# Conv units as pairs of seven block products; gate and silu units beside the S5 layer

## The chip, the cores and the metric

One core of a Trainium2 chip runs one layer of a hybrid encoder on a sequence of 1024 tokens of width 1024, in fp32. The metric is the device time of one execution in microseconds (us). Before the change it is 1185.5 us, the median of three runs (1178.62, 1185.71 and 1185.5).

## The reference

The inner width of every unit is 1024. `u` goes through the S5 layer, 64 groups of 16 channels with complex diagonal states in both directions:

```
xn = RMSNorm(x)
u, z_a, v, b, c, z_b, g_a, g_b = split(xn @ W_in)          # eight units, 1024 x 1024 each
y  = gelu(S5(u));  y = y * sigmoid(y @ W_glu);  y_a = y * silu(z_a)
y_b = b * conv3(c * v) * silu(z_b)                          # 3 taps along the sequence
merged = sigmoid(g_a) * (y_a @ W_branch_a) + sigmoid(g_b) * (y_b @ W_branch_b)
out = RMSNorm(x + merged @ W_out)
```

## The kernel before

**Products.** An fp32 operand is kept as two fp32r tiles, a high part and the rest (`split`, L817: a CAST on ACT, a subtraction on DVE). A product of 128 output channels by 1024 positions is three passes (high x high, high x low, low x high) over eight blocks of 128 input channels and two halves of 512 positions: 48 matmuls of 128x512. Its weights are one load of 512 KB (`load_w`, L112).

**Pairs of seven.** Two neighbouring products (256 channels) can also be done as seven block products instead of eight (Strassen's scheme in Winograd's form): `seven` (L920 on) does B11, T2, T1, T3, B21, B22 and T4, 12 matmuls each, 84 instead of 96. For it the positions need sums and differences of blocks of xn (`sh`, `sl`, made once, L848 to L858), and the weights differences (`diff`, L899) that are split again; `prep` makes them for the next pair while this one runs. DVE's adds (`plus`, L943) put the products together in the tiles `go`. Each product has a PSUM tile of its own, from the pool `bg` of single banks (`bank`).

**Stages.** A prologue (norm, transposes, S5 tables, four units of `u`); then 46 products one after the other (`items`, run by `projections`), four for `u`, 32 for the conv (`conv_tile`: v, c, b and zb of each of eight channel blocks, finished on DVE and ACT right behind each), eight for za and two for gb; then seven pairs (the six other blocks of gb, all of ga); then the products ob, glu, oa and o.

**S5.** Between the products' blocks of six matmuls, S5's work is put in where a planner says that it is due: `ssm` yields one step at a time, `est` keeps its estimates of PE's and DVE's time, `part` queues a piece of PE work with the time from which it may go. Blocks n = 0 to 15 (four groups each) pass through: loads of U, bdt and pwt (512 KB each for the last two) and four DVE operations make the input map; `xps`, small matmuls, brings its product with U into SB; after four blocks, a scan of DVE operations (L666, L670); then `output_block` loads `ce`, makes W with six DVE operations (L618 to L620), `kf` and `kb` (L633, L636) make the kernel of the block, four small transfers `toe` turn it, and `yps` writes the output.

**Orders that matter below.** Each engine takes its instructions in the order of the program; SP issues all transfers in its own order, and an issue that waits holds those behind it. A tile of a pool is given again when its earlier use is over, and the program waits for that.

Of the kernel before, what the change touches and what calls it, by code (L numbers as in the profile page):

```python
# [52 lines left out]
def block_kernel(  # L53
# [46 lines left out]
    zsd = [dtile(f"zsd{i}", [P, D]) for i in range(K)]  # L100
    ctd = dtile("ctd", [P, NG // 4 * 192])
# [62 lines left out]
    with ExitStack() as st:  # L164
# [76 lines left out]


        def small(name, dt=F32, n=P):
            return pp.tile([NG, n], dt, tag=name, name=name)
# [6 lines left out]
        braw, craw = [], []  # L251
        for ri, (b, c) in enumerate(((ssm_b_re, ssm_c_re), (ssm_b_im, ssm_c_im))):
            bt = pp.tile([NG, 2, NG, H], F32, tag=f"braw{ri}", name=f"braw{ri}")
            nc.sync.dma_start(out=bt.rearrange("g d p h -> g d (p h)"), in_=b[0].rearrange("d g p h -> g d (p h)"))
            braw.append(bt)
            ct = pp.tile([P, K, 2, NG], F32, tag=f"craw{ri}", name=f"craw{ri}")
# [4 lines left out]
            craw.append(ct)  # L261
# [103 lines left out]
        Q = pp.tile([P, T + 1, 2, NG], F32, tag="Q", name="Q")  # L365
# [5 lines left out]
        qt1 = pp.tile([P, 4, NG], F32, tag="qt1", name="qt1")  # L371
        qt2 = pp.tile([P, 4, NG], F32, tag="qt2", name="qt2")
# [12 lines left out]
        Ein = pp.tile([P, T, 2, NG], F32, tag="Ein", name="Ein")  # L385
# [9 lines left out]
        bt1 = pp.tile([P, 8, NG], F32, tag="bt1", name="bt1")  # L395
        bt2 = pp.tile([P, 8, NG], F32, tag="bt2", name="bt2")
# [17 lines left out]
        R = pp.tile([P, L, 2, NG], F32, tag="R", name="R")  # L414
# [93 lines left out]
    def ssm(sp):  # L508
# [13 lines left out]
        def input_block():  # L522
            n = at["n"]
            q = n // 4
            if n % 4 == 0:
                SBs[q] = sp.tile([P, P, 2, GQ], F32, tag="SB", name=f"SB{q}", bufs=2)
# [4 lines left out]
            for src, outer, tag in ((bd, [[NG * 2 * P, H], [0, T]], "bdt"), (pw, [[0, H], [NG * 2 * P, T]], "pwt")):  # L531
                r_ = sp.tile([P, 4, 2, P], F32, tag=tag, name=f"{tag}_{nm}", bufs=2)
# [31 lines left out]
        def lags(b):  # L564
# [27 lines left out]
            b["out"] = part(est["dve"] + 4.0, 2.7, out_)  # L592

        def output_block(n, SB):
            gl = 4 * (n % 4)
            nm = f"y{n}"
            U = load_u(n, nm)
# [10 lines left out]
            Sx = sp.tile([P, 4, 2, P], F32, tag="Sx", name=f"Sx_{nm}")  # L608
            zsrc = SB[:, :, :, gl:gl + 4].rearrange("p k r g -> p g r k")
            G.memset(Sx[0:NG, :, :, 0:1], 0.0)  # L610
            G.memset(Sx[NG:P, :, :, P - 1:P], 0.0)
            S.copy(out=Sx[0:NG, :, :, 1:P], in_=zsrc[0:NG, :, :, 0:P - 1])  # L612
            S.copy(out=Sx[NG:P, :, :, 0:P - 1], in_=zsrc[NG:P, :, :, P - 2::-1])
# [9 lines left out]
            b = dict(nm=nm, n=n, U=U, Sx=Sx, W=W, out=None,  # L623
# [59 lines left out]
        def outputs():  # L683
            bs = []
            for n in range(NG // 4):
                while n // 4 not in scanned:
                    if bs and "done" not in bs[-1] and ready(bs[-1]["part"], 1.2):
                        lags(bs[-1])
                        bs[-1]["done"] = True
                        yield True  # L690
                    else:
                        yield False
                while len(bs) > 1 and not (bs[-2]["out"] and bs[-2]["out"]["end"] is not None):
                    yield False
                bs.append(output_block(n, SBs[n // 4]))
                if n % 4 == 3:
                    put_out.add(n // 4)
                yield True
                for b in bs[-2:] if n == NG // 4 - 1 else bs[-2:-1]:
                    while not ready(b["part"], 1.2):  # L700
                        yield False
                    if "done" not in b:
                        lags(b)
                        b["done"] = True
                    yield True
# [3 lines left out]
        while alive:  # L709
            for w in list(alive):  # L710
# [17 lines left out]
    def keep_u(i):  # L728
        def done(ps):
            us = t4(f"us{i}")  # L730
            S.copy(out=us, in_=ps)
            nc.sync.dma_start(out=ud[i], in_=us)
        return done

    def conv_tile(i):
        live = {}

        def v(ps):
            live["v"] = vs = t4(f"vs{i}")
            S.copy(out=vs, in_=ps)  # L740

        def c(ps):
            cv = t4(f"cv{i}")
            vec(5.3)
            V.tensor_tensor(out=cv, in0=ps, in1=live["v"], op=ALU.mult)
            live["acc"] = acc = t4(f"acc{i}")
            S.activation(out=acc, in_=cv, func=AF.Identity, scale=col(2, i), bias=col(4, i))
            w0, w2 = col(1, i), col(3, i)
            for w, do, so, n in ((w0, P, 0, 7 * P), (w0, 1, 7 * P, P - 1), (w2, 0, P, 7 * P), (w2, 7 * P, 1, P - 1)):
                V.scalar_tensor_tensor(out=acc[:, do:do + n], in0=cv[:, so:so + n], scalar=w,  # L750
                                       in1=acc[:, do:do + n], op0=ALU.mult, op1=ALU.add)

        def b(ps):
            vec(1.18)
            V.tensor_tensor(out=live["acc"], in0=ps, in1=live["acc"], op=ALU.mult)

        def zb(ps):
            sg, acc = t4(f"sgb{i}"), live["acc"]
            vec(3.0)
            S.activation(out=sg, in_=ps, func=AF.Sigmoid)  # L760
            V.tensor_tensor(out=sg, in0=ps, in1=sg, op=ALU.mult)
            V.tensor_tensor(out=acc, in0=acc, in1=sg, op=ALU.mult)
            nc.sync.dma_start(out=ybd[i], in_=acc)

        return [(wcol(2, i), v), (wcol(4, i), c), (wcol(3, i), b), (wcol(5, i), zb)]

    def za(i):
        def done(ps):
            sg = t4(f"sga{i}")
# [3 lines left out]
            nc.sync.dma_start(out=zsd[i], in_=sg)  # L773
# [7 lines left out]
    def gb(i):  # L781
        def done(ps):
            sg = t4(f"sgb{i}")
            S.activation(out=sg, in_=ps, func=AF.Sigmoid)
            nc.sync.dma_start(out=gbd[i], in_=sg)
        return done

    items += [(wcol(7, i), gb(i)) for i in range(2)]

    def projections():  # L790
        pair, done = load_w(items[0][0], "p0"), None
        for n, (w, next_done) in enumerate(items):
            ps = mm_tile(f"ps_p{n}")
            for k in range(K):
# [7 lines left out]
                if n + 1 == len(items) and k:  # L802
                    if k == 1:
                        late["first"] = load_pair(0)
                    elif 2 <= k <= 6:
                        while "S" not in late:
# [21 lines left out]
    late = {}  # L828
# [3 lines left out]
    def beside():  # L832
        with ExitStack() as own:
            sp = own.enter_context(tc.tile_pool(name="sp", bufs=2))
            yield from ssm(sp)
            while parts and not flush[0]:
                yield False
            put_parts(True)
        tabs.close()
        late["st"] = gs = ExitStack()  # L840
        sx = gs.enter_context(tc.tile_pool(name="sx", bufs=1))
        late["sw"] = gs.enter_context(tc.tile_pool(name="sw", bufs=1))
        late["S"] = {n: [] for n in "1234"}
        for k in range(HK):
            xs = []
# [5 lines left out]
            yield True  # L851
            for names, ops in (("31", ((xs[0], 0, xs[0], 1, ALU.subtract), (xs[0], 1, xs[1], 1, ALU.add))),
                               ("24", ((None, 1, xs[0], 0, ALU.subtract), (xs[1], 0, None, 0, ALU.subtract)))):
# [4 lines left out]
                h_ = sx.tile([P, D], F32R, tag=f"h{names}_{k}", name=f"sh{names}_{k}")  # L858
                l_ = sx.tile([P, D], F32R, tag=f"l{names}_{k}", name=f"sl{names}_{k}")
# [6 lines left out]
        for k in range(2):  # L866
            yt = t4(f"ybt{k}")
            nc.sync.dma_start(out=yt, in_=ybd[k])
            hi = tuple(xnh[2 * k + h][:, half[1]] for h in range(2))
            lo = tuple(xnl[2 * k + h][:, half[1]] for h in range(2))  # L870
            for h in range(2):
                split(yt[:, half[h]], hi[h], lo[h])
                vec(0.66)
            ybh.append(hi)
            ybl.append(lo)
            yield True

    pairs7 = [(7, i) for i in range(2, K, 2)] + [(6, i) for i in range(0, K, 2)]
# [17 lines left out]
    def diff(p, w, name, x_, y_):  # L896
        f_ = late["sw"].tile([P, HK, P], F32, tag="f4" if name == "T4" else "tf", name=f"f{name}_{p}",
                             bufs=1 if name == "T4" else 3)
# [27 lines left out]
    def seven(p, w):  # L926

        sx = late["S"]
# [239 lines left out]
```

## Time and profile before

| what | us |
|---|---|
| median of three runs | 1185.5 |
| the profiled execution | 1183.82 |
| its span | 1182.1 |
| PE busy | 1144.2 (97%) |
| DVE busy | 773.6 (65%) |
| ACT busy | 452.1 (38%) |
| mean granted TensorE clock | 0.993 of full speed |

All times are microseconds of one profiled execution. Busy is the union of an engine's instructions. In a timeline a row has its start, its length, engine, source line and operation, output and inputs, and in brackets how long the engine had stood idle before it and what ended that. The chain of waits follows the work that ended last back from the end. Matmuls are pipelined: a row of PE lasts longer than the distance to the next one.

### The profile page before, as it was taken

The page shows a single profiled execution, that of the slowest core. Times are in us where ns is not written, and L with a number is a line of the kernel's source. Part 1 is how long each engine was busy: PE and PEld are TensorE (multiplying, and loading weights), DVE is VectorE, ACT ScalarE, POOL GpSimd, SP SyncE. Part 2 cuts the span into 40 slices and gives each one's busy share as a digit, 9 for nine tenths or more (in the row PEclk, how much of TensorE's full clock was granted, in tenths as well). Part 3 has the DMA queues.
Part 4 walks back from the last instruction along what each step waited for, and adds up shares of the span by engine and source line. Part 5 has one row for each costly group of instructions (what it writes and reads, how often), then busy time and mean ns, then how long its engine had stood idle before and what let it go on. Part 6 is the DMA issues. An engine that isn't in the chain of part 4 may idle for free.

```text
span 1182.1 us, 14984 instructions
## 1 busy us (share of the span) xinstructions
PE 1144.2 (97%) x5842; PEld 948.1 (80%) x5842; DVE 773.6 (65%) x1220; ACT 452.1 (38%) x541; POOL 14.5 (1%) x59
## 2 busy tenths in 40 slices
PE   6999999998999999999999999999999999999997
PEld 4778888877788888878888878888788888887886
DVE  6854698884889959877955876564477325446244
ACT  6344752455314571433164343433344224223111
POOL 2000000000000000000000000000000000000000
PEclk9999999999999999999999999999999999999999
DMA  9249962146522462233344233427667424227012
GB/s 273 87 142 288 250 182 72 48 131 169 139 67 65 120 164 72 66 104 104 107 115 116 89 107 125 143 72 244 235 193 255 156 91 159 90 72 267 1 49 95
DMA packets 162427, 157.31 MB, mean 133 GB/s; under 512 B 11404, under 2 KB 138548, under 8 KB 162228
## 3 DMA queue, kind: packets, MB, share of 16 engines
q1 hardware_dynamic: 162212, 156.16, 43.3%
q8 instruction: 46, 0.75, 0.3%
q14 instruction: 25, 0.20, 0.0%
q10 hardware_dynamic: 144, 0.20, 0.0%
HBM read 114.39 MB, written 37.75 MB: 129 GB/s over the span
## 4 chain that ended last, share of the span: by engine, by line
PE 83%; DVE 6%; DMA 4%; ACT 3%; issue 2%; SPq 1%; POOL 0%; POOLq 0%; ACTq 0%; DVEq 0%
PE ps_p L134 35%; PE ps_glu L134 7%; PE o L1115 7%; PE ps_oa L134 7%; PE ps_ob L134 7%; PE gT L937 6%; PE gB L937 5%; PE xps_x L554 2%; PE ps_u L134 2%; PE yps_y L584 1%; PE yps_y L583 1%; PE yps_y L582 1%; DVE s L856 1%; DVE sl L819 1%; ACT sh L818 1%
## 5 line engine op out<-in xcount | busy, mean ns | idle before, releaser
L134 PE MATMUL ps_p<-xnh,wh_p 128*128 128x512 f32 x736 | 231.5, 396 | 0.0
L134 PE MATMUL ps_p<-xnl,wh_p 128*128 128x512 f32 x736 | 227.5, 390 | 0.0
L134 PE MATMUL ps_p<-xnh,wl_p 128*128 128x512 f32 x736 | 227.0, 390 | 0.0
L134 PEld LDWEIGHTS ps_p<-xnl,wh_p 128*128 128x128 f32 x736 | 138.4, 188 | 29.4
L134 PEld LDWEIGHTS ps_p<-xnh,wl_p 128*128 128x128 f32 x736 | 138.4, 188 | 29.1
L134 PEld LDWEIGHTS ps_p<-xnh,wh_p 128*128 128x128 f32 x736 | 135.4, 188 | 28.9 <-issue 3.2
L117 ACT CAST wh_p<-wr_p 128x1024 fp32r<-128x1024 f32 x46 | 48.4, 1053 | 175.8 <-PE ps_p L134 107.9
L670 DVE TENSOR_TENSOR SB<-SB,st 128x32 f32<-128x32 f32 (+2 forms) x232 | 98.7, 425 | 8.0
L666 DVE TENSOR_TENSOR st<-SB,ac 128x64 f32<-128x64 f32 (+2 forms) x116 | 80.0, 690 | 8.5 <-DMA ac<-acd 5.6
L1115 PE MATMUL o<-wo,mh 128*128 128x512 f32 (+1 forms) x272 | 81.0, 382 | 1.4 <-ACT mh L818 1.4
L118 DVE TENSOR_TENSOR wl_p<-wr_p,wh_p 128x1024 fp32r<-128x1024 f32 x46 | 56.0, 1217 | 24.7 <-ACT wh_p L117 24.7
L1115 PEld LDWEIGHTS o<-wo,mh 128*128 128x128 f32 x272 | 50.7, 191 | 11.6 <-ACT mh L818 1.9
L1115 PE MATMUL o<-wo,ml 128*128 128x512 f32 (+1 forms) x136 | 52.1, 383 | 0.3 <-DVE ml L819 0.3
L542 DVE TENSOR_TENSOR g_x<-bdt_x,pwt_x 128x1024 f32<-128x1024 f32 x16 | 19.6, 1223 | 47.1 <-DMA bdt_x<-bd 29.5
L943 DVE TENSOR_TENSOR go<-gT,go 128x512 f32<-128x512 f32 x35 | 23.5, 687 | 37.9 <-PE gT L937 17.9
L557 ACT COPY SB<-xps_x 64x512 f32<-64x512 f32 x32 | 35.1, 1098 | 23.6 <-PE xps_x L554 23.2
L612 ACT COPY Sx_y<-SB 64x1016 f32<-64x1016 f32 x16 | 34.0, 2123 | 22.0 <-DVE SB L670 21.8
L554 PE MATMUL xps_x<-U_x,bdt_x 128*128 128x128 f32 x256 | 33.5, 287 | 9.1 <-issue 5.0
L554 PEld LDWEIGHTS xps_x<-U_x,bdt_x 128*128 128x128 f32 x256 | 32.5, 202 | 11.1 <-issue 6.2
L134 PE MATMUL ps_oa<-yal,wh_oa 128*128 128x512 f32 x128 | 39.5, 390 | 0.0
L134 PE MATMUL ps_oa<-yah,wh_oa 128*128 128x512 f32 x128 | 39.4, 389 | 0.0
L134 PE MATMUL ps_glu<-ygh,wh_glu 128*128 128x512 f32 x128 | 39.4, 389 | 0.0
(295 smaller groups left out, 2034.9 us busy)
## 6 DMA issues: line engine op xcount, KB each, us to landing
wr_p<-in_w_in_dram SPq DMA_DIRECT2D x46, 512.0 KB
bdt_x<-bd SPq DMA_DIRECT2D x16, 512.0 KB
pwt_x<-pw SPq DMA_DIRECT2D x16, 512.0 KB
x<-in_x_dram SPq DMA_DIRECT2D x8, 512.0 KB
ud<-us SPq DMA_DIRECT2D x8, 512.0 KB
U_x<-ud SPq DMA_DIRECT2D x16, 256.0 KB
U_y<-ud SPq DMA_DIRECT2D x16, 256.0 KB
ybd<-acc SPq DMA_DIRECT2D x8, 512.0 KB
```

The costliest lines, as they stand in the source:

```text
L117: S.copy(out=hi, in_=raw)
L118: V.tensor_tensor(out=lo, in0=raw, in1=hi.bitcast(F32), op=ALU.subtract)
L134: nc.tensor.matmul(out=ps[:, 512 * h:512 * h + 512], lhsT=l[:, k, :], rhs=r[k][h] if isinstance(r[k], tuple) else r[k][:, 512 * h:512 * h ...
L542: V.tensor_tensor(out=g_, in0=Wi, in1=er, op=ALU.mult)
L554: nc.tensor.matmul(out=xps[:, P * j:P * j + P], lhsT=Wi[:, j, ri, :], rhs=U[:, j, :], start=True, stop=True)
L557: S.copy(out=dst[0:NG], in_=x3[0:NG])
L612: S.copy(out=Sx[0:NG, :, :, 1:P], in_=zsrc[0:NG, :, :, 0:P - 1])
L666: V.tensor_tensor(out=t_[:, 0:n].rearrange("p b r s g -> p b r (s g)"), in0=bcast(z.rearrange("p b r g -> p b (r g)"), 2, 2), in1=bcast(ac ...
L670: V.tensor_tensor(out=o, in0=o, in1=t_[:, 0:n, :, s_], op=ALU.add)
L937: nc.tensor.matmul(out=ps, lhsT=w[n][l][:, k, :], rhs=xs[k][r], start=k == 0 and i == 0, stop=k == HK - 1 and i == 2)
L943: V.tensor_tensor(out=out, in0=ps, in1=in_, op=ALU.add)
L1115: nc.tensor.matmul(out=ps[:, 0:n], lhsT=l[:, ts_], rhs=r, start=(k == 0 and i == 0), stop=(k == K - 1 and i == 2))
```

## The change

The items beside S5 are now 36 products: four of u; gb and za in turn, eight each, each stored as soon as it is there (gb as sigmoid, za raw); eight of zb, with its silu stored in `zbd`, with six of ga between them; and v's first two blocks, stored in `vd`. The pairs are now twelve: c and b of blocks 0 and 1, then v, c and b of blocks 2 and 3, 4 and 5, 6 and 7, and the last pair of ga. The conv itself (`later_c`, `later_b`) is cut into jobs, one of which is put on DVE and ACT behind each block product; zb comes back from HBM in four transfers a triple. The silu of za moves to the products of glu.

```
-    items = [(wcol(0, i), keep_u(i)) for i in range(K // 2, K)]
-    for i in range(K):
-        items += conv_tile(i)
-    items += [(wcol(1, i), za(i)) for i in range(K)]
-    items += [(wcol(7, i), gb(i)) for i in range(2)]
+    NGA = 6
+    items = [(wcol(0, i), keep(ud[i])) for i in range(K // 2, K)]
+    for i in range(K):
+        items += [(wcol(7, i), sigm(gbd[i])), (wcol(1, i), keep(zsd[i]))]
+    for i in range(K):
+        items.append((wcol(5, i), silu(zbd[i])))
+        if i < NGA:
+            items.append((wcol(6, i), sigm(gad[i])))
+    items += [(wcol(2, i), keep(vd[i])) for i in range(2)]
...
-    pairs7 = [(7, i) for i in range(2, K, 2)] + [(6, i) for i in range(0, K, 2)]
+    pairs7 = [(u, i) for i in range(0, K, 2) for u in (2, 4, 3)][1:] + [(6, i) for i in range(NGA, K, 2)]
```

In `seven`, T1 and T3 now share one PSUM tile of two banks, T4 has another, from the pool of the full products; the other four keep single banks. In the loop over a pair's products, a job follows the next pair's preparation and stands ahead of the add of the product just issued:

```
-        def prod(n, xs):
-            ps = bank(f"g{n}_{p}")
+        wide = {}
+        def prod(n, xs, place=None):
+            if place is None:
+                ps = bank(f"g{n}_{p}")
+            else:
+                if place[0] not in wide:
+                    wide[place[0]] = mm_tile(f"gw{place[0]}_{p}")
+                ps = wide[place[0]][:, half[place[1]]]
...
-        g = prod("T1", sx["1"])
+        g = prod("T1", sx["1"], (0, 0))
         yield 2
-        plus(at(1, 0), g, at(0, 1))
-        g = prod("T3", sx["3"])
+        plus(1, 0, g, at(0, 1))
+        g = prod("T3", sx["3"], (0, 1))
...
                 if nxt and n:
                     prep(p + 1, nxt, n)
+                if jobs:
+                    jobs.pop(0)()
...
+    def later_c(i, cv, v):
+        def by_v(q):
+            V.tensor_tensor(out=cv[q], in0=cv[q], in1=v[q], op=ALU.mult)
+        def begin(q):
+            accs[q] = t4(f"acc{i + q}")
+            S.activation(out=accs[q], in_=cv[q], func=AF.Identity, scale=col(2, i + q), bias=col(4, i + q))
+        def taps(q, w):
...
+        jobs.extend([first, lambda: by_v(1), lambda: taps(0, 1), fourth, lambda: taps(1, 1), lambda: taps(1, 3)])
...
+    def later_b(i, yb):
+        def gate(q):
+            V.tensor_tensor(out=yb[q], in0=yb[q], in1=accs[q], op=ALU.mult)
...
+        jobs.extend([lambda: gate(0), lambda: end(0), lambda: gate(1), lambda: end(1)])
```

In `ssm` the output block is cut in two: `output_map` (ce, W, kf, kb) may be made before the scan that its block needs has ended, for two blocks ahead, and `states` (U, Sx) follows the scan. S5's larger tiles (SB, bdt, pwt) and the tables' now lie in one pool `turn_p`, whose space then goes to the combinations of xn (`combinations`); those of two of the four block rows are made before S5 ends.

```
+            while n < NG // 4 or live:
+                for b in live:
+                    if "there" not in b and b["n"] // 4 in scanned:
+                        states(b)
...
+                elif len(live) < 2 and n < NG // 4 and est["pe"] >= 8.0:
+                    live.append(output_map(n))
+                    n += 1
+                    yield True
```

In the products of glu:

```
         nc.sync.dma_start(out=zt, in_=zsd[i])
+        sz = t4(f"sz{i}")
+        S.activation(out=sz, in_=zt, func=AF.Sigmoid)
...
+        V.tensor_tensor(out=zt, in0=zt, in1=sz, op=ALU.mult)
         V.tensor_tensor(out=zt, in0=zt, in1=y_, op=ALU.mult)
```

The order of instructions shows three places. The first is PE in a pair, where T3 follows T1. Before (pair 2; `gT1` and `gT3` are the PSUM tiles, `sh31` and `sl31` the combinations of xn, `hT` and `lT` the split differences of weights):

```order
L937 MATMUL gT1_2_6038<-sh31_2_5556,hT1_2_5950 128x512
L937 MATMUL gT1_2_6038<-sl31_2_5557,hT1_2_5950 128x512
L937 MATMUL gT1_2_6038<-sh31_2_5556,lT1_2_5951 128x512
L937 MATMUL gT1_2_6038<-sh31_3_5614,hT1_2_5950 128x512
L937 MATMUL gT1_2_6038<-sl31_3_5615,hT1_2_5950 128x512
L937 MATMUL gT1_2_6038<-sh31_3_5614,lT1_2_5951 128x512
L937 MATMUL gT3_2_6056<-sh31_0_5402,hT3_2_5971 128x512 [waits DVE_49,Activation_49]
L937 MATMUL gT3_2_6056<-sl31_0_5403,hT3_2_5971 128x512
L937 MATMUL gT3_2_6056<-sh31_0_5402,lT3_2_5972 128x512
```

And now (pair 4, b of blocks 2 and 3; `gw0` is the tile of two banks, `sx` the combinations):

```order
L931 MATMUL gw0_4_5697<-sx2_4935,lT1_4_5608 128x512
L931 MATMUL gw0_4_5697<-sx3_4990,hT1_4_5607 128x512 x2
L931 MATMUL gw0_4_5697<-sx3_4990,lT1_4_5608 128x512
L931 MATMUL gw0_4_5697<-sx0_0_4562,hT3_4_5627 128x512 [waits DVE_49,Activation_49]
L931 MATMUL gw0_4_5697<-sx0_1_4563,hT3_4_5627 128x512
L931 MATMUL gw0_4_5697<-sx0_0_4562,lT3_4_5628 128x512
L931 MATMUL gw0_4_5697<-sx1_4837,hT3_4_5627 128x512 x2
L931 MATMUL gw0_4_5697<-sx1_4837,lT3_4_5628 128x512
```

The output of T3's matmuls was another tile than T1's, and is now the same tile; T3's first matmul has waits on DVE and ACT in both.

The second place is DVE in the same stretch. Before, between the add of T2 and that of T1 stood two differences for the next pair (`fT1`, `fT2`):

```order
L943 TENSOR_TENSOR go1_0_5857<-gT4_1_5979,go1_0_5857 128x512
L819 TENSOR_TENSOR lT4_2_6016<-fT4_2_5975,hT4_2_6015 128x512
L943 TENSOR_TENSOR go2_0_6000<-gT2_2_6024,go2_0_6000 128x512
L899 TENSOR_TENSOR fT1_3_6051<-wr_b3_6021,wr_a3_6019 128x512
L899 TENSOR_TENSOR fT2_3_6053<-wr_b3_6021,fT1_3_6051 128x512
L943 TENSOR_TENSOR go2_1_6001<-gT1_2_6038,go2_0_6000 128x512
L819 TENSOR_TENSOR la_3_6070<-wr_a3_6019,ha_3_6069 128x1024
L819 TENSOR_TENSOR lT2_3_6074<-fT2_3_6053,hT2_3_6073 128x512
```

Now (pair 4) two operations of the conv's taps (`acc2`, on `go3_0`, the product c times v) stand behind them and ahead of the add that reads T1:

```order
L986 TENSOR_TENSOR go3_0_5516<-go3_0_5516,v2_5373 128x1024
L986 TENSOR_TENSOR go3_1_5517<-go3_1_5517,v3_5374 128x1024
L937 TENSOR_TENSOR go4_0_5655<-gT2_4_5682,go4_0_5655 128x512
L886 TENSOR_TENSOR fT1_5_5710<-wr_b5_5676,wr_a5_5674 128x512
L886 TENSOR_TENSOR fT2_5_5712<-wr_b5_5676,fT1_5_5710 128x512
L995 SCALAR_TENSOR_TENSOR acc2_5679<-go3_0_5516,cols_215,acc2_5679 128x896
L995 SCALAR_TENSOR_TENSOR acc2_5679<-go3_0_5516,cols_215,acc2_5679 128x127
L937 TENSOR_TENSOR go4_1_5656<-gw0_4_5697,go4_0_5655 128x512
L807 TENSOR_TENSOR la_5_5730<-wr_a5_5674,ha_5_5729 128x1024
```

The add that reads T1 has moved back by one job. In the pairs that follow a pair of b (those of v, and the last) the job there is a multiplication of 128x1024 instead (`gate`), and in those that follow v (those of c) there is none.

The third place is PE in the second product beside S5. Before, its first S5 work was `xps` of block 0, in the third product:

```order
L134 MATMUL ps_p2_1113<-xnl1_157,wh_p2_1061 128x512 x2
L134 MATMUL ps_p2_1113<-xnh1_149,wl_p2_1062 128x512 x2
L554 MATMUL xps0_x0_1135<-U_x0_1090,bdt_x0_1092 128x128 [waits DMAHW1_49,DMAHW3_49,DMAHW0_49,DMAHW7_49,DVE_49,Pool_49]
L554 MATMUL xps0_x0_1135<-U_x0_1090,bdt_x0_1092 128x128 x3
L554 MATMUL xps1_x0_1142<-U_x0_1090,bdt_x0_1092 128x128 [waits DVE_49]
L554 MATMUL xps1_x0_1142<-U_x0_1090,bdt_x0_1092 128x128 x3
```

Now the kernel of output block 0 (`kf_y0`, `kb_y0`) comes after 12 matmuls of the second product (`ps_p1`), 60 after the first product began:

```order
L136 MATMUL ps_p1_1057<-xnh1_162,wl_p1_1002 128x512 x2
L649 MATMUL kf_y0_1092<-W_y0_1034,Bt_158 32x128 [waits DMAHW3_49,DMAHW7_49,DVE_49,Activation_49]
L652 MATMUL kb_y0_1093<-W_y0_1034,Bt_158 32x128 [waits Activation_49]
L649 MATMUL kf_y0_1092<-W_y0_1034,Bt_158 32x128
L652 MATMUL kb_y0_1093<-W_y0_1034,Bt_158 32x128
L649 MATMUL kf_y0_1092<-W_y0_1034,Bt_158 32x128
L652 MATMUL kb_y0_1093<-W_y0_1034,Bt_158 32x128
L649 MATMUL kf_y0_1092<-W_y0_1034,Bt_158 32x128
L652 MATMUL kb_y0_1093<-W_y0_1034,Bt_158 32x128
```

So `W_y0`, made from `ce_y0` and so from the table `ctd` that the prologue stores, is now wanted 42 matmuls ahead of `xps` of block 0, where before it was first wanted far behind it. By the same rules `xps` of block 10, which followed that of block 9 with nothing between, now has two stretches of 12 matmuls, one of 24 and two of 16 small ones of `kf` and `kb` between.

## Rows read from the trace of the kernel before

**Rows 1.** Busy time on the page: engine, busy us, share of the span, instructions

```profile
PE 1144.2 (97%) x5842; PEld 948.1 (80%) x5842; DVE 773.6 (65%) x1220; ACT 452.1 (38%) x541; POOL 14.5 (1%) x59
```

**Rows 2.** Windows by stage: stretch, us, busy us by engine, granted clock, DMA share, GB/s

```profile
79.70:682.10 602.40, 590.79 (x3361) 493.85 (x3360) 452.96 (x690) 260.09 (x271) 3.41 (x32) 0.99 0.45 125
682.10:819.60 137.50, 135.49 (x589) 111.44 (x589) 83.01 (x124) 51.84 (x80) 0.00 (x0) 0.99 0.40 130
...
907.80:995.10 87.30, 87.30 (x387) 72.29 (x386) 35.26 (x32) 22.26 (x23) 0.00 (x0) 1.00 0.43 149
```

**Rows 3.** Chain of waits, T2, T1 and T3 of second and fourth pair: start, us, what

```profile
708.47 8.16 PE gT L937 x36
...
746.55 8.16 PE gT L937 x36
```

**Rows 4.** Timeline of the fourth pair: DVE and one matmul of PE

```profile
749.37 0.69 DVE L943 TENSOR_TENSOR go<-gT,go 128x512 f32<-128x512 f32 x1 [4.21 <-issue]
...
750.69 0.69 DVE L899 TENSOR_TENSOR fT<-wr_b,fT 128x512 f32<-128x512 f32 x1
...
752.03 0.69 DVE L943 TENSOR_TENSOR go<-gT,go 128x512 f32<-128x512 f32 x1 [0.65 <-PE gT L937]
752.06 0.39 PE L937 MATMUL gT<-sl,hT 128*128 128x512 f32 x1
```

**Rows 5.** Chain of waits, first pair: between the end of `sl` on DVE and PE

```profile
689.75 0.04 issue
```

**Rows 6.** Groups of DVE by form, 100 to 660: busy, mean ns, idle before

```profile
L750 DVE SCALAR_TENSOR_TENSOR acc<-cv,cols,acc 128x896 f32<-128x896 f32 x16 | 18.4, 1152 | 12.1 <-ACT acc L747 11.8
...
L745 DVE TENSOR_TENSOR cv<-ps_p,vs 128x1024 f32<-128x1024 f32 x8 | 9.7, 1218 | 0.4 <-PE ps_p L134 0.4
...
L750 DVE SCALAR_TENSOR_TENSOR acc<-cv,cols,acc 128x127 f32<-128x127 f32 x16 | 5.5, 346 | 0.0
```

**Rows 7.** Timeline of DVE in the second pair: a late load

```profile
714.76 0.69 DVE L899 TENSOR_TENSOR fT<-wr_b,wr_a 128x512 f32<-128x512 f32 x1 [2.78 <-DMA wr_b<-in_w_in_dram]
...
716.09 0.68 DVE L943 TENSOR_TENSOR go<-gT,go 128x512 f32<-128x512 f32 x1
```

**Rows 8.** Chain of waits, start of the products beside S5

```profile
80.09 24.48 PE ps_p L134 x108
```

**Rows 9.** Timeline: the store of `ctd` (SPq, its queue), and one operation of W

```profile
82.73 0.40 SPq L473 DMA_DIRECT2D ctd<-CE  x1
...
227.67 0.68 DVE L618 TENSOR_TENSOR W_y<-ce_y 128x512 f32<-128x512 f32 x1
```

**Rows 10.** Windows inside and just behind the stage with S5

```profile
80.00:130.00 50.00, 49.55 (x245) 41.68 (x244) 19.79 (x20) 21.86 (x21) 0.42 (x4) 1.00 1.00 285
...
230.00:310.00 80.00, 71.91 (x495) 60.42 (x494) 56.20 (x74) 42.40 (x50) 0.85 (x8) 0.96 0.54 143
...
420.00:430.00 10.00, 8.12 (x45) 6.73 (x44) 3.43 (x4) 5.91 (x6) 0.00 (x0) 1.00 0.93 243
...
690.00:700.00 10.00, 10.00 (x38) 8.07 (x38) 6.41 (x10) 4.54 (x8) 0.00 (x0) 0.83 0.47 159
```

**Rows 11.** Chain of waits, blocks 10 and 11 of S5

```profile
278.59 8.10 DMA bdt_x<-bd
...
290.19 2.62 PE xps_x L554 x16
...
299.29 2.67 issue
```

**Rows 12.** Timeline of PE in the first pair's T2

```profile
688.53 0.50 PE L937 MATMUL gT<-sh,hT 128*128 128x512 f32 x1 [1.25 <-ACT sh L818]
689.79 0.51 PE L937 MATMUL gT<-sl,hT 128*128 128x512 f32 x1 [0.76 <-DVE sl L819]
...
690.82 0.63 PE L937 MATMUL gT<-sh,lT 128*128 128x512 f32 x1
...
694.23 0.40 PE L937 MATMUL gT<-sl,hT 128*128 128x512 f32 x1
```

More of the change, by code (lines that the diff above doesn't have):

```diff
@@ L503, in put_parts, with ssm @@
             p_["end"] = est["pe"]
-    def ssm(sp):
+    def ssm(sp, other):
         def ready(p_, us):
@@ L683, in outputs @@
         def outputs():
[L684 to L693, printed above, removed]
-                    yield False
[L695 to L705, printed above, removed]
+            live, n = [], 0
+            while n < NG // 4 or live:
+                for b in live:
+                    if "there" not in b and b["n"] // 4 in scanned:
+                        states(b)
+                        if b["n"] % 4 == 3:
+                            put_out.add(b["n"] // 4)
+                    if b["out"] is None and "last" in b and "there" in b:
+                        b["out"] = part(max(b["ready"], b["there"]), 2.7, b["last"])
+                if live and live[0]["out"] and (live[0]["out"]["end"] is not None or flush[0]):
+                    live.pop(0)
+                now = [b for b in live if "last" not in b and ready(b["part"], 1.2)]
+                if now:
+                    lags(now[0])
+                    yield True
+                elif len(live) < 2 and n < NG // 4 and est["pe"] >= 8.0:
+                    live.append(output_map(n))
+                    n += 1
+                    yield True
+                else:
+                    yield False
         alive = [outputs(), inputs(), scans()]
         while alive:
-            for w in list(alive):
+            late["go"] = 2 if 2 in put_out else int(at["n"] == NG // 4)
+            for w in alive + [other]:
                 got = next(w, None)
@@ L805, in projections @@
                     elif 2 <= k <= 6:
-                        while "S" not in late:
+                        while late["go"] < HK:
                             flush[0] = True
@@ L827, in block_kernel, with combinations @@
     ybh, ybl = [], []
-    late = {}
+    late = {"go": 0}
     HK = K // 2
     half = (slice(0, 512), slice(512, D))
[L832 to L842, printed above, removed]
+    def combinations():
         late["S"] = {n: [] for n in "1234"}
         for k in range(HK):
+            while late["go"] <= k:
+                yield False
+            if k == 0:
+                to = [turn_p.tile([P, D], F32R, tag=f"X{j}", name=f"sx0_{j}") for j in range(4)]
+            else:
+                y_ = (turn_p if k < 3 else late["sx"]).tile([P, 4, D], F32R, tag=f"Y{k - 1}", name=f"sx{k}")
+                to = [y_[:, j] for j in range(4)]
             xs = []
@@ L865, in beside @@
                 yield True
[L866 to L876, printed above, removed]
-    pairs7 = [(7, i) for i in range(2, K, 2)] + [(6, i) for i in range(0, K, 2)]
+    def beside():
+        own_s = combinations()
+        with ExitStack() as own:
+            sp = own.enter_context(tc.tile_pool(name="sp", bufs=2))
+            yield from ssm(sp, own_s)
+            while parts and not flush[0]:
+                yield next(own_s)
+            put_parts(True)
+        tabs.close()
+        late["st"] = gs = ExitStack()
+        late["sx"] = gs.enter_context(tc.tile_pool(name="sx", bufs=1))
+        late["sw"] = gs.enter_context(tc.tile_pool(name="sw", bufs=1))
+        late["go"] = HK
+        yield from own_s
+    pairs7 = [(u, i) for i in range(0, K, 2) for u in (2, 4, 3)][1:] + [(6, i) for i in range(NGA, K, 2)]
     def load_pair(p):
@@ L979, in gates @@
     def gates():
         w = late["first"]
+        for q in range(2):
+            vs.append(held(q, f"v{q}"))
+            nc.sync.dma_start(out=vs[q], in_=vd[q])
         for p in range(len(pairs7)):
```

204 lines of the change are left out of this document (114 added, 90 removed).

## The prediction

> **What bounds the kernel now.** I read the busy times first: PE works for 1144.2 us of a span of 1182.1 [rows 1], so it is the resource, and what the other engines do counts only where PE waits for it. The windows by stage show where it waits [rows 2]: 11.6 us are lost in the stage with S5 (602.4 long, 590.8 busy), none in the products of glu. Then the price of a matmul: in the chain of waits 36 follow one another in 8.16 us, 0.2267 each, without a stop [rows 3]. So a plain product is 48 x 0.2267 = 10.88 us, a pair of seven 84 x 0.2267 = 19.04, against 21.76 for two plain products.
>
> **The arithmetic of the change.** Before: 46 plain products and 7 pairs, 46 x 48 + 7 x 84 = 2796 matmuls. After: 36 and 12, 36 x 48 + 12 x 84 = 2736. That takes 60 x 0.2267 = 13.6 us from PE. S5's own matmuls, the prologue and the last four products stay as they are. This is all that the change can give by doing less; the rest is waits.
>
> **T3 behind the add of T1: +16.3.** T1 and T3 now are two halves of one tile. If the program waits by tile, T3's first matmul may write only when the add that reads T1 has been done. Before, they were two tiles, and the rows show the overlap: in the fourth pair T3's first matmul starts at 751.83 (the one printed is its second, 752.06, 0.23 behind), and the add that reads T1 only at 752.03 [rows 4]. Nothing else on PE can fill the place, since PE takes its instructions in order, and B21 stands behind T3.
>
> How late is the add? DVE's queue [rows 4]: T2's add at 749.37, two differences, the second at 750.69, idle from 751.38, T1's add at 752.03 for 0.69, so done at 752.72. With 0.04 from DVE's end to PE, as between `sl` and the matmul behind it [rows 5], T3 could start at 752.76, 0.93 behind its 751.83. That holds where no job is in the way: five pairs (the four of c, and the last, where there is nothing to prepare and the job has its room). In the three pairs of v, behind a pair of b, the job is one multiplication of 128x1024, 1.22 us [rows 6]: from 751.38 it is done at 752.60, the add at 753.29, T3 at 753.33, 1.50 late. In the four pairs of b, behind a pair of c, it is two operations of 1.15 and 0.35 [rows 6]: 752.88, 753.57, 753.61, 1.78 late. Sum: 5 x 0.93 + 3 x 1.50 + 4 x 1.78 = 16.3. Its lower end is nothing, if the dependence is by bank after all. For the upper end there is a row of before: in the second pair DVE waited 2.78 us for the load `wr_b`, and T1's add began only at 716.09 [rows 7], ended at 716.77. T3's place there is 708.47 + 5.28 = 713.75 (in the fourth pair 746.55 + 5.28 [rows 3, 4]), so the add was 3.0 late. That was harmless, since nobody waited; in the changed kernel it would hold PE, and twelve times 3.0 is 36. I don't take it: there the load stood behind the stores of a pair of gates on SP's queue, and now most pairs store nothing.
>
> The Trainium skill (PSUM — Partial Sum Buffer, section "PSUM bank collisions raise a hardware error") wants engines kept apart by bank: a matmul into one bank may run while VectorE reads another. A half of 512 fp32 is a bank there, so by that rule the wait is not needed, and without it this term were nothing. The trace agrees as far as it goes: the add read T1's tile while T3 wrote another [rows 4].
>
> **The early W: +4.** `kf_y0` now comes 60 matmuls after the products begin. The first product begins at about 79.9, since 108 matmuls from 80.09 take 24.48 us [rows 8]; 60 x 0.2267 makes 93.6. Its W needs `ctd`, 1.5 MB, which SP issues at 82.73 [rows 9], then a load of `ce`, then two small copies on ACT and six operations on DVE like that of 227.67, 0.68 each, 4.1 us [rows 9]. The DMA moves 285 GB/s in this stretch at a share of 1.00 [rows 10]: `ctd` alone is 5.5 us at that rate, so done at 88 to 90, and the load queues behind other stores and weights, 2 to 5 us. With 0.5 for the copies W_y0 is there between 94.6 and 99.6, and PE waits 1 to 6; the second W two stretches on adds 0 to 1.5. A part is given back: `xps` of block 0 in turn waited 0.45 for its operands and comes at the 102nd matmul in place of the 108th. I take +4, with 1 to 8 as ends.
>
> **Blocks 9 to 11 and other stops of S5: -7.** From 230 to 310 PE was busy 71.91 of 80 us, so 8.1 idle, at a mean clock of 0.96 [rows 10]. The chain shows what: `bdt` for block 10 is issued at 278.59, lands 8.10 later, and DVE's four operations bring `xps` to 290.19; then another 2.67 ahead of block 11, for which no releaser is shown [rows 11]. `xps` of block 10 stood directly behind that of block 9. Now 48 matmuls of products stand between, 10.9 us, and two W are made early, which also takes the wait for W out of the start of that stretch. I give back 6 of 8.1, and 1 of the 1.9 that PE lost between 420 and 430 [rows 10]; the low clock would go as well, up to 2 more, which I don't count. Bounds: 0 (the stop moves to another block, for the loads are as many) and -12.
>
> **More traffic early: +1.** Every product beside S5 now stores 512 KB, 36 stores for 36 products; before, 22 for 46 products, with the conv's three silent products between. In the first 50 us the DMA is full, so loads for blocks 4 to 7 may come later. Bounds 0 and 12.
>
> **The rest: 0.** The silu of za in the glu products is 8 x 1.22 on DVE [rows 6] and about as much on ACT, where DVE is busy 35.26 of 87.3 us and PE never waits [rows 2]; without that cover it were 10. Conv taps and gates move from DVE beside S5 to DVE beside the pairs: in a pair of b 2 x 1.22 + 4 x 1.50 = 8.4 us [rows 6], on top of the pair's own sixteen operations of 128x512 (0.69 [rows 4]) and one of 1.22, 12.3: 20.7 in the 20.8 us of a pair with its stop. DVE fits, with nothing to spare; if it doesn't, the excess shows as a longer stop. Two of the four block rows of combinations are made early; the last two still end behind S5, so I leave the first pair's loss as it is, 137.5 - 7 x 19.04 = 4.2 us [rows 2]: idle 1.25 and 0.76, then matmuls 0.43 apart instead of 0.23 [rows 12]. The reloads of zb and v are 5 MB in some 230 us, where the DMA's share in the pairs was 0.40 [rows 2].
>
> **Sum.** From the profiled execution's 1183.8 (1.7 below the median, 0.14%): -13.6 + 16.3 + 4 - 7 + 1 = +0.7, 1184.5. I say **1184**. What a measurement of this kernel can tell from no change is about 1%, 1173.6 to 1197.4.
>
> **The rivals.**
> *The wait is not there, or is covered.* If T3 does not wait for T1's add, the sum is 1184 - 16 = 1168; half of it, with S5's losses all regained (-12 instead of -7), gives 1171. For it: two tiles need no such wait [rows 4]. Against it: in the code both halves come from one tile, and the order shows T3's first matmul with a wait on DVE. Chance 0.22 with its mixtures.
> *The stops bring the clock down: slower.* In the first pair two stops, 1.25 and 0.76, were followed by matmuls at about half the pace: from 690.82 to 694.23, 3.41 us, eight matmuls [rows 12], where 1.81 would do, so 1.6 lost; the granted clock of that window, 0.83 [rows 10], mixes the two levels, 1.2 and 2.4 GHz. If each of the twelve stops does this, 19 us: 1203. It decides if more than eight do. Against it: between 420 and 430 PE idled 1.88, more than any of my stops (0.93 to 1.78), and the clock stayed at 1.00 [rows 10]. The Trainium skill (TensorE: Matmul & The Clock Gate, section "A second HAM failure mode: psum-queue depth-cycling") tells of a kernel whose short idles between groups of matmuls, from the cycling of PSUM banks, made the clock swing; by that rule this rival would be the forecast; the trace does not agree, for after the 1.88 us the clock held. Chance 0.12.
> *Loads late: slower.* If `wr_b` still lands late in half of the pairs (3.0 instead of 0.93 to 1.78, some 1.5 more each, 9; a backlog on DVE would look the same) and blocks 4 to 7 stop by 2 each (8), 1184 + 17 = 1201; either alone 1192. Chance of over 1197: 0.12.
> Forecast with its own range, 1174 to 1197: 0.54.
>
> Chances: faster by over 1% 0.22, within 1% 0.54, slower 0.24. The range for 8 in 10 is 1168 to 1202.
>
> **What would show it.** Right: a wait of PE on DVE's add ahead of T3 in all twelve pairs, 0.9 to 1.8 us each, B11 to B11 20.0 to 20.8 us; PE busy about 1131 to 1135; a stop of some us ahead of `kf_y0` near 93; less than 3 us idle between blocks 8 and 11; granted clock 1.00 through the pairs. Wrong: T3 following T1 at 0.23 (first rival), a clock under 1 in windows of the pairs (second), waits of DVE for `wr_b` or of PE for `bdt` (third).

## The result, and the profile after

The changed kernel takes 1188.3 us against 1180.9 before, medians of 20 runs each: a ratio of 1.0059, 95% interval 1.0042 to 1.0076. It is slower, by 7.0 us as the ratio gives it (the medians are 7.4 apart); the forecast was 1184, no change that one could tell. All medians and ratios here are of fast runs. In twenty runs the kernel before is 4.6 us faster than the median of three that was shown, and its profiled execution (1183.8) lies 2.9 above the new median. The profiled execution after took 1184.2, 4.1 below its median. So the two traces stand 0.4 apart: they show where time is lost, but not the whole of the 7 us.

PE has the fewer matmuls and is less busy, and the span is as long. The page after, busy times (before: [rows 1]):

```profile
PE 1132.7 (96%) x5782; PEld 935.1 (79%) x5782; DVE 818.7 (69%) x1303; ACT 462.4 (39%) x556; POOL 14.4 (1%) x59
```

Where PE waits, in all, after (engine, line, releaser: us, times, longest):

```profile
PE gw L931 <- DVE go L937: 10.2, 9, 1.5
PE xps_x L566 <- DVE bdt_x L556: 5.2, 2, 4.3
PE gw L931 <- DVE v L937: 3.9, 3, 1.3
PE gT L931 <- ACT sx L806: 2.5, 1, 2.5
PE kf_y L649 <- DVE W_y L636: 1.4, 1, 1.4
PE kf_y L649 <- issue: 1.4, 1, 1.4
...
PE xps_x L566 <- DMA U_x<-ud: 1.2, 1, 1.2
```

The twelve waits of `gw` for DVE's adds are T3's, 14.1 us. The others shown are S5's, in the first 100 us beside the products (`kf`, and `xps` for `bdt`) and once ahead of block 9 (`xps` for `U`), and the first pair's (`gT` for `sx`).

Windows after: the first 100 us beside S5, the stretch of blocks 8 to 11, the first pair, and the eleven other pairs (stretch, us, busy by engine, granted clock, DMA share, GB/s):

```profile
80.00:180.00 100.00, 91.96 (x511) 76.49 (x510) 60.53 (x72) 53.18 (x55) 0.43 (x4) 0.97 0.90 245
230.00:310.00 80.00, 78.82 (x535) 66.42 (x535) 65.08 (x120) 41.93 (x51) 0.85 (x8) 1.00 0.67 183
570.00:597.50 27.50, 23.51 (x89) 18.19 (x88) 17.67 (x25) 7.96 (x12) 0.00 (x0) 0.88 0.32 98
597.54:823.08 225.54, 212.27 (x926) 172.58 (x925) 172.59 (x248) 62.81 (x89) 0.00 (x0) 1.00 0.31 96
```

The first of them of the kernel before:

```profile
80.00:180.00 100.00, 99.55 (x504) 84.52 (x503) 63.31 (x72) 52.16 (x51) 0.42 (x4) 1.00 0.89 242
```

So 0.45 us idle in the first 100 have become 8.04, and 8.09 between 230 and 310 [rows 10] have become 1.18. The eleven pairs last 225.54, where 11 x 19.04 = 209.4 would do: 16.1 lost, at a clock of 1.00.

One pair of c (the fourth) on the chain of waits, after, and DVE in it. In the chain T2, T1, the add, T3 and on to the next pair's B11:

```profile
641.63 2.72 PE gT L931 x12
644.35 2.73 PE gw L931 x12
...
647.11 0.70 DVE go L937
647.81 0.14 issue
...
647.94 2.96 PE gw L931 x12
...
659.07 2.72 PE gB L931 x12
```

```profile
644.46 0.69 DVE L937 TENSOR_TENSOR go<-gT,go 128x512 f32<-128x512 f32 x1 [4.22 <-PE gT L931]
645.07 0.68 DVE L886 TENSOR_TENSOR fT<-wr_b,wr_a 128x512 f32<-128x512 f32 x1
645.78 0.69 DVE L886 TENSOR_TENSOR fT<-wr_b,fT 128x512 f32<-128x512 f32 x1
647.11 0.69 DVE L937 TENSOR_TENSOR go<-gw,go 128x512 f32<-128x512 f32 x1 [0.64 <-PE gw L931]
```

This is the picture of [rows 4], with the one difference that T3 now starts behind the add of 647.11 and not beside it. The pair lasts from 638.91 to 659.07, 20.16 us, 1.12 more than 19.04. A pair of b lasts 20.80 (from 597.54 to 618.34) and one of v 20.57 (618.34 to 638.91): these are the starts of B11 on the chain:

```profile
597.54 2.72 PE gB L931 x12
...
618.34 2.72 PE gB L931 x12
...
638.91 2.72 PE gB L931 x12
```

### The profile page after: what moved, and what is told of

The parts are those of the page before. It is cut to its first block, busy times and chain, and to the rows that moved or that the text cites. A ratio compares the mean times of both kernels' runs of the same rounds, so it can differ in the third digit from the quotient of the medians.

```text
span 1182.4 us, 15042 instructions
## 1 busy us (share of the span) xinstructions
PE 1132.7 (96%) x5782; PEld 935.1 (79%) x5782; DVE 818.7 (69%) x1303; ACT 462.4 (39%) x556; POOL 14.4 (1%) x59
## 4 chain that ended last, share of the span: by engine, by line
PE 85%; DVE 6%; DMA 4%; issue 2%; ACT 2%; SPq 0%; POOL 0%; POOLq 0%; DVEq 0%; ACTq 0%
PE ps_p L136 30%; PE gB L931 8%; PE ps_glu L136 7%; PE gw L931 7%; PE o L1181 7%; PE ps_oa L136 7%; PE ps_ob L136 7%; PE gT L931 3%; PE ps_u L136 2%; PE xps_x L566 2%; DMA bdt_x<-bd 2%; PE yps_y L596 1%; PE yps_y L595 1%; PE yps_y L594 1%; DVE fT L886 1%
## 5 line engine op out<-in xcount | busy, mean ns | idle before, releaser
L136 PE MATMUL ps_p<-xnh,wh_p 128*128 128x512 f32 x576 | 182.1, 398 | 0.0
L136 PE MATMUL ps_p<-xnl,wh_p 128*128 128x512 f32 x576 | 178.1, 390 | 0.0
L136 PE MATMUL ps_p<-xnh,wl_p 128*128 128x512 f32 x576 | 177.8, 390 | 0.0
L136 PEld LDWEIGHTS ps_p<-xnl,wh_p 128*128 128x128 f32 x576 | 108.5, 188 | 23.1
L136 PEld LDWEIGHTS ps_p<-xnh,wl_p 128*128 128x128 f32 x576 | 108.4, 188 | 23.0
L136 PEld LDWEIGHTS ps_p<-xnh,wh_p 128*128 128x128 f32 x576 | 105.9, 189 | 22.9 <-issue 3.2
L931 PE MATMUL gw<-sx,hT 128*128 128x512 f32 x192 | 61.9, 405 | 14.0 <-DVE go L937 10.2
L931 PEld LDWEIGHTS gw<-sx,hT 128*128 128x128 f32 x192 | 36.2, 194 | 26.1 <-ACT hT L806 16.3
L136 PE MATMUL ps_oa<-yah,wl_oa 128*128 128x512 f32 x128 | 39.4, 389 | 0.0
L136 PE MATMUL ps_glu<-ygh,wl_glu 128*128 128x512 f32 x128 | 39.4, 389 | 0.0
```

The source lines that it names most:

```text
L136: nc.tensor.matmul(out=ps[:, 512 * h:512 * h + 512], lhsT=l[:, k, :], rhs=r[k][h] if isinstance(r[k], tuple) else r[k][:, 512 * h:512 * h ...
L931: nc.tensor.matmul(out=ps, lhsT=w[n][l][:, k, :], rhs=xs[k][r], start=k == 0 and i_ == 0, stop=k == HK - 1 and i_ == 2)
```

## The experiments

Each kernel was timed beside the kernel before on the same chip, and differences to the changed kernel go by the two ratios, times 1181 us.

**T1 and T3 in two tiles.** T1 and T4, which stand apart in time, share one wide tile; T3 has the other.

```
-        g = prod("T3", sx["3"], (0, 1))
+        g = prod("T3", sx["3"], (1, 0))
...
-        g = prod("T4", A(HK, 1), (1, 0))
+        g = prod("T4", A(HK, 1), (0, 1))
```

> The changed kernel with T1 and T3 in two wide tiles (T1 and T4 share one, T3 has the other); the same work. Theory A (T3's wait for the add of T1 is the whole loss of the pairs): in the trace after the change the pairs follow one another at 20.16, 20.6 and 20.8 us in place of 19.04, some 17.2 us in all; all of it goes, pairs come to 19.1 each and the time from 1188 to about 1171, ratio to before 0.992. Rival B (DVE is full in the four pairs of b: 20.7 us of work by its operations' durations): without the stop these four pairs stay at 20 to 20.7 and the stop moves to another place behind DVE; gain only 10 to 12, about 1177. Rival C (the stops are covered by other waits): no gain.

Measured: 1171.7, ratio 0.9924 (0.9903 to 0.9945), so 1.35% or 15.9 us below the changed kernel, and faster than the kernel before. The chain of waits shows T1 and T3 without a stop, and from B11 to B11 (658.11 to 677.15) 19.04 us:

```profile
641.79 2.72 PE gT L931 x12
644.51 5.44 PE gw L931 x24
649.95 5.44 PE gB L931 x24
655.39 2.72 PE gw L931 x12
658.11 2.72 PE gB L931 x12
...
677.15 2.72 PE gB L931 x12
```

The eleven pairs behind the first are all like that, those of b too. So the rivals fall: DVE, with 20.7 us of operations by their lengths, holds nobody up within 19.04. Sums of its lengths count too much: in the timeline above the row of 0.69 at 644.46 is followed by the next after 0.61 (the third, which reads what the second wrote, comes 0.71 behind it).

**The add ahead of the job.** The same tile for T1 and T3, but T1's add written ahead of the next pair's differences and of the job:

```
         g = prod("T1", sx["1"], (0, 0))
-        yield 2
         plus(1, 0, g, at(0, 1))
+        yield 2
```

> The changed kernel with the add that reads T1 written ahead of the next pair's differences and the job, T1 and T3 still in one tile; the same work. Theory A (the stop is the wait for that add, longer by what stands ahead of it on DVE): all twelve stops come to the shortest, pairs of 20.1 to 20.2 us, 17.2 - 12 x 1.1 = 4 us faster, about 1184. Rival B (DVE's backlog, not its order, sets the stop in the pairs of b and v): these stay at 20.6 to 20.8, no gain.

Measured: 1182.1, ratio 1.0012 (0.9997 to 1.0027), 5.5 us below the changed kernel; 4 were expected, within the intervals. Pairs of all kinds now have the short stop; two starts of B11 on the chain are 20.16 apart:

```profile
640.66 2.72 PE gB L931 x12
...
660.82 2.72 PE gB L931 x12
...
680.99 2.72 PE gB L931 x12
```

So what stood ahead of the add on DVE is the difference between 20.16 and 20.6 or 20.8, and the rest, some 1.1 a pair, is the wait for the add itself.

**The shared tile in the kernel before.** T1 and T3 of its seven pairs as halves of one wide tile, as the change has them, and nothing else.

> The kernel before with one edit: T1 and T3 of its seven pairs as halves of one wide tile. Theory A: a stop in each pair: five of 0.93 plus 0.2 for the restart, and 3.2 and 2.1 in the second and third pair, where DVE waits for a late load ahead of the add: 11 us slower, ratio 1.009. Rival: no change, if PE does not stop for the add there.

Measured: 1193.6, ratio 1.0113 (1.0092 to 1.0135): 13.3 us slower, 11 expected. The total is met in part by luck. Five of the waits are short ones (0.87 or 0.88), those of the second and third pair too, for which 3.2 and 2.1 were expected. The sixth is in the first pair, where DVE's queue stood behind a split that waited for a late load (`ybt`, which this kernel puts there). In the seventh pair four matmuls of ob stand in the stop's place. On the chain, the first pair:

```profile
689.05 6.09 DMA ybt<-ybd
...
699.63 0.61 DVE go L949
700.29 4.34 PE gw L943 x12
```

So the wait is the tile's and not the conv's or the jobs', and it lends PE every lateness of DVE: this one was 5.9 us by the list of waits.

**The first output maps later.** In the changed kernel, the planner may make them from 60 us of its time on, in place of 8; `kf` of block 0 then follows `xps` of block 5:

```
-                elif len(live) < 2 and n < NG // 4 and est["pe"] >= 8.0:
+                elif len(live) < 2 and n < NG // 4 and est["pe"] >= 60.0:
```

> The changed kernel with the first output maps allowed from 60 us of the planner's time in place of 8, so that kf of block 0 comes behind xps of block 5; the same work. Theory A (the wait for W at 93 to 97 us is a loss by itself): the stop of 3 to 4 us and the lower clock behind it go, 4 to 5 us faster, about 1184. Rival B (the transfers of the first 100 us are the bound, and PE only waits at another place): xps of blocks 0 to 7 wait the same time more, no gain, 1187 to 1189.

Measured: 1182.5, ratio 1.0015 (0.9999 to 1.0032), 5.2 us below the changed kernel. The expectation's size is met, but the trace tells more: PE idles 2.45 us of the first 100 in place of 8.04, so the stops ahead of blocks 5 and 7 (0.89 and 4.33) went too, which neither theory said, and all that is left is ahead of block 0; and S5 ends a product later, so that the combinations of xn come late to the first pair:

```profile
80.00:180.00 100.00, 97.55 (x545) 82.41 (x544) 61.68 (x73) 54.94 (x57) 0.43 (x4) 0.98 0.94 257
```

```profile
PE gT L931 <- ACT sx L806: 9.1, 2, 7.5
```

Here 9.1 us stand where the changed kernel waited 2.5. Some 6.6 us were given back there.

**Less traffic early.** Six stores (gb and za of the first three blocks, 3 MB) are left out of the first 120 us beside S5; later the first three blocks of ga are stored in their places too.

```
-        items += [(wcol(7, i), sigm(gbd[i])), (wcol(1, i), keep(zsd[i]))]
+        early = i < 3
+        items += [(wcol(7, i), sigm() if early else sigm(gbd[i])), (wcol(1, i), keep(None if early else zsd[i]))]
...
-            items.append((wcol(6, i), sigm(gad[i])))
+            items.append((wcol(6, i), sigm(gad[i], gbd[i], zsd[i]) if i < 3 else sigm(gad[i])))
```

> The changed kernel without the six stores of gb's and za's first three blocks (3 MB in the first 120 us beside S5); later the three first blocks of ga are stored in their places too, so the later work has its loads, with other data. Theory A (the stops ahead of xps of blocks 6 and 7 at 150 to 180 us, some 5 us and a low clock, come from more traffic): they go, 6 to 7 us faster, 1181 to 1182. Rival B (they come from the order: blocks 6 and 7 stand 42 and 18 matmuls earlier than in the kernel before, their loads are issued when a slot's earlier block has been used): they stay, 1187 to 1189, and only the first stop at kf is shorter.

(The expectation miscounts: block 6, like block 7, stands 18 matmuls earlier than before, 270 in place of 288, and the stops of the changed kernel are ahead of blocks 5 and 7.) Measured: 1185.3, ratio 1.0028 (1.0015 to 1.0041), 3.7 us below the changed kernel, between the two theories. PE still idles 7.06 of the first 100:

```profile
80.00:180.00 100.00, 92.94 (x513) 77.22 (x512) 58.52 (x70) 53.97 (x57) 0.42 (x4) 0.97 0.86 233
```

So the added stores can be a part at most, and the larger one is left to the order. Where the 3.7 us were gained this trace doesn't show: only 1.0 of them are idle time of this stretch, and the clock is the same. The stores were also not only taken away, but put in later.

**Both edits, and two other places for the maps.** T1 and T3 apart, and the first maps from 60, 20 and 46 us of the planner's time on.

> The changed kernel with both edits: T1 and T3 in two wide tiles, and the first output maps from 60 us of the planner's time on; the same work. If the two losses are separate they add: 16.6 and 5.7 us measured alone, 1188.3 - 22.3 = 1166, ratio to before 0.987. If shorter pairs leave DVE or the transfers short, less than 16.6 shows, 1170 or more.

> As the kernel with T1 and T3 apart, and the first output maps from 20 us of the planner's time: kf of block 0 comes 12 matmuls behind xps of block 0, and all S5 work behind it stands where it stood in the changed kernel, so S5 ends as early as there. Theory A (the stop at kf is a loss of its own): 4 us faster than with T1 and T3 apart, 1167 to 1168, stops ahead of xps of blocks 6 and 7 as in the changed kernel. Rival B (blocks 0 to 7 of S5 wait for transfers, and a stop ahead of kf only takes a part of that wait): the stops of blocks 1 to 7 grow by as much, 1171 to 1172.

> The changed kernel with T1 and T3 in two wide tiles and the first output maps from 46 us of the planner's time: xps of blocks 0 to 3 stand where they stood in the kernel before, kf of block 0 behind that of block 3, and S5 ends as early as in the changed kernel. If the early stop is the place of W among the first loads, and the late end of S5 what the kernel with 60 us lost again (7.1 us ahead of the first pair's T2), both go: 1167 - 4 = 1162 to 1163. If blocks 4 to 7 then wait for loads, 1166 as with 20 us.

Measured: 1167.3, ratio 0.9883 (0.9865 to 0.9900); 1166.1, 0.9871 (0.9852 to 0.9890); 1162.2, 0.9824 (0.9804 to 0.9844). The first two losses add, as expected (1166). With 20, PE idles 6.23 us of the first 100 and the long stop has moved to 130 to 140, ahead of other blocks, so it is neither of the two theories clean. With 46, `xps` of blocks 0 to 3 stand as in the kernel before and S5 ends as early as in the changed kernel; the early idle is 4.04 and the first pair waits 2.5 as in the changed kernel:

```profile
80.00:180.00 100.00, 95.96 (x537) 80.52 (x536) 63.53 (x75) 54.54 (x57) 0.42 (x4) 0.98 0.91 255
```

This is the fastest version: 1.8% faster than the kernel before, 2.35% faster than the changed one, with the places of T3 and T4 and one threshold changed. From the kernel with T3 apart alone (0.9924) to this one are 11.8 us. Most of what the traces show of that is in the first 100 us, which in the kernel with T3 apart alone read:

```profile
80.00:180.00 100.00, 90.43 (x498) 74.77 (x498) 57.03 (x68) 52.77 (x58) 0.43 (x4) 0.95 0.90 241
```

That is 5.5 us more of idle time, at a lower clock. It is not the whole price of the early maps and the traffic, since 4.04 are still idle.

**Block 10 further behind block 9, in the kernel before.**

```
-            at["t"] = max(at["t"], est["pe"] - 6.0) + 8.0
+            at["t"] = max(at["t"], est["pe"] - 6.0) + (16.0 if n == 9 else 8.0)
```

> The kernel before with one edit to the planner: 16 us in place of 8 between the input blocks 9 and 10 of S5, so that xps of block 10 stands 24 matmuls behind that of block 9 and that of block 11 another 30, and nothing else moves. Theory A (the change's gain in S5 came from this place): the 6.7 us that PE stood idle between 280 and 310, and the low clock behind, go: 6 to 8 us faster, about 1174, ratio 0.994. Rival B (the stop follows the loads to another place): no gain, or less than 2.

Measured: 1173.3, ratio 0.9917 (0.9900 to 0.9934): 9.8 us faster, more than expected. The stretch that idled 8.09 at a mean clock of 0.96 [rows 10] now idles 1.41 at 1.00:

```profile
230.00:310.00 80.00, 78.59 (x540) 66.15 (x539) 64.79 (x88) 47.44 (x53) 0.85 (x8) 1.00 0.57 152
```

The same stretch in the changed kernel has 78.82 busy and 1.00, so the new order of S5 gave as much there; whether it did so by block 10 alone was not tried in that kernel. The first 100 us, where nothing was changed, show how far one execution differs from another: 2.48 us idle ahead of block 0 at a clock of 0.98, where the profile of the kernel before has 0.45 at 1.00.

```profile
80.00:180.00 100.00, 97.52 (x488) 83.07 (x487) 60.76 (x65) 52.18 (x51) 0.43 (x4) 0.98 0.87 237
```

## Why the prediction was right or wrong

**The arithmetic, -13.6: right as far as it goes.** 60 matmuls are gone, and every pair without a stop takes 19.04 (T1 and T3 apart).

**T3 behind the add, +16.3: right.** 15.9 us by the two ratios; in the trace 16.1 in eleven pairs and 1.1 in the first. By kind: 1.12 where 0.93 was said, 1.53 (20.57 - 19.04) for 1.50, 1.76 (20.80 - 19.04) for 1.78. The short stop is longer since from DVE's end to T3 it is 0.14 and not 0.04, and since T3's first matmuls stand further apart, which makes another 0.09 (rows in the last section). The waits for late loads, the upper end, did not come in these pairs. By the Trainium skill (PSUM — Partial Sum Buffer, section "PSUM bank collisions raise a hardware error") engines need guarding against each other within a bank, not across banks. The kernel had the wait all the same: its program waits by tile, and the time went with the tile (T1 and T3 apart) and came with it (the kernel before).

**The early maps and the traffic, +4 and +1: this step failed.** The two terms say 5; the runs show 10 to 12. In the traces the first 100 us idle 7.6 more than before, and a clock of 0.97 for 1.00 costs some 3 more (an estimate, 0.03 of 100). By the ratios of the two kernels with T3 apart it is 11.8, with 4.04 still idle there. The step priced the first stop, ahead of `kf`, and this is how the chain after has it:

```profile
83.20 7.40 DMA ctd<-CE
...
90.75 2.58 DMA ce_y<-ctd
...
97.43 0.42 PE kf_y L649
```

PE waits 2.8 us there, within the 1 to 6 that were said. What was not counted is behind it: with `kf` put ahead of `xps` of block 0, most input blocks stand 6 to 18 matmuls earlier than before (blocks 6 and 7 by 18), in a stretch where the DMA has little room (a share of 0.90), and PE came to stops (0.89 ahead of block 5, 4.33 ahead of block 7, in the timeline). The chain after has the loads of `bdt` for blocks 6 and 7, 11.64 and 6.19 us from issue to landing:

```profile
144.80 11.64 DMA bdt_x<-bd
...
162.04 6.19 DMA bdt_x<-bd
```

Then the clock, which the step left out: it fell behind the two stops ahead of `kf`, and again behind that of block 7 (0.83 from 170 to 180).

```profile
90.00:100.00 10.00, 7.17 (x56) 5.12 (x55) 6.47 (x11) 3.57 (x8) 0.43 (x4) 0.86 0.91 281
```

I had the bound of 12 for blocks 4 to 7 and took 1. That the order is the larger part is shown by the maps at 60 (idle 2.45 with all the stores) and by the stores left out (7.06 with fewer); how much each of the stops takes over from the others is not. About half of the 11.8 may be clock: over the runs of these two kernels its median is 0.991 with the early maps and 0.996 with the maps from 46 on, and 0.005 of 1181 us is 5.9 (an estimate).

**Blocks 9 to 11, -7: right in place, too small.** -9.8 by the kernel before with block 10 moved. I took 6 of 8.1 us there (and 1 elsewhere) and left the low clock out. In the trace after 6.9 are gone, and the clock is back at 1.00 from 0.96 (another 3.2, 0.04 of 80).

**The first pair, 0: wrong by some 2.5.** The waits for `sx` are 2.52 and 0.69 in place of 1.25 and 0.76 [rows 12], in the timeline of PE after:

```profile
573.43 0.62 PE L931 MATMUL gT<-sx,hT 128*128 128x512 f32 x2
...
578.15 0.57 PE L931 MATMUL gT<-sx,hT 128*128 128x512 f32 x1 [2.52 <-ACT sx L806]
579.41 0.79 PE L931 MATMUL gT<-sx,hT 128*128 128x512 f32 x1 [0.69 <-DVE sx L807]
```

T2 begins at 573.43, so B11 at 570.71, and the next B11 at 597.54: 26.8, 7.8 above 19.04, of which 1.1 are T3's stop; it was 4.2 before. This was read from the two traces, not tried, and why the last `sx` come later there stays open.

**The sum.** -13.6 + 15.9 + 11.8 - 9.8 + 2.5 = +6.8, against 7.0 measured. That it comes so close is luck: 15.9, 11.8 and 9.8 come from ratios with intervals of 2 to 2.5 us to either side. The forecast's +0.7 missed by 6.8 in the early stretch and 2.5 in the first pair, and had 2.8 too little from blocks 9 to 11 and 0.4 too much for T3.

The two profiled executions alone would not have refuted it. Up to the first B11 the one after takes 490.3 us (80.4 to 570.7) and the one before 602.4 [rows 2]; with ten products of 10.88 less, that is 3.3 better, and 2 were forecast (4 + 1 - 7). The early loss of 10.6 is made up there by 10.1 at blocks 9 to 11 and some 4 elsewhere in S5, among them the 1.9 between 420 and 430 [rows 10]. The rest of the 7 us lies in executions that were not profiled, and no run shows where. A hint is the granted clock: its median is 0.990 over the twenty runs after (0.993 in the profiled one), and 0.993 to 0.995 where the kernel before ran beside the experiments; 0.003 of 1181 us would be 3.5 (an estimate).

**The rivals.** The clock did not fall behind T3's stops: the stops were 0.9 to 1.5 us, and the granted clock was 1.00 over the eleven pairs. So what the Trainium skill (TensorE: Matmul & The Clock Gate, section "A second HAM failure mode: psum-queue depth-cycling") tells of short idles between groups of matmuls in another kernel is not borne out in the pairs. In the early stretch, where the forecast did not look for it, the clock did fall. The rival of late loads had the right half, blocks 4 to 7 (it priced them at 8), and a wrong one, `wr_b`. The signs that the forecast named for itself came, the stop ahead of `kf` and 1.00 through the eleven pairs among them; but so did one that it named against itself, PE's waits for `bdt`, 5.2 us in all.

## What to carry to other kernels

Put two results into one PSUM tile only if the second is not wanted while the first is still to be read; a tile of two banks that is waited for as one costs the reader's time at every use. When a planner's threshold moves one small job ahead of others, look at what the others' loads then meet: the first stop is not the whole price. And before rebuilding a stage, try moving the one block that stops it: 16 in place of 8 in one line of the kernel before gave 9.8 us, not far from the 13.6 that 60 matmuls less can give.

## What the runs showed of the hardware that was not expected

After a stop for DVE's add, T3's matmuls began 0.14 us behind the add's end (in the first pair 0.05), where `sl` and its matmul had 0.04 [rows 5]; and from the first to the third of them it was 0.54 in place of 0.45 (647.94 and 648.48):

```profile
646.68 0.39 PE L931 MATMUL gw<-sx,lT 128*128 128x512 f32 x1
647.94 0.70 PE L931 MATMUL gw<-sx,hT 128*128 128x512 f32 x2 [0.88 <-DVE go L937]
648.48 0.39 PE L931 MATMUL gw<-sx,lT 128*128 128x512 f32 x1
```

T3 begins 1.26 behind the last matmul of T1, 1.03 more than the 0.23 without a stop. With the other 0.09, a stop that the profile gives as 0.88 us costs 1.12. And stops like these, 0.88 to 1.5 us and one every 20 us, left the granted clock at 1.00, while 1.40 and 1.43 ahead of `kf`, one close behind the other, were followed by a fall (0.86 from 90 to 100), and the first pair's 2.52 and 0.69 by a window at 0.74:

```profile
580.00:590.00 10.00, 9.22 (x30) 6.97 (x29) 4.98 (x7) 1.24 (x2) 0.00 (x0) 0.74 0.02 6
```
